# Low parts of split weights: a scaled copy on ScalarE and an accumulating transfer in place of a subtraction

## The chip, the cores and the metric

One of the eight cores of a Trainium2 chip runs the whole program. The metric is device time in microseconds (us) of one execution; the number given is the median of three runs.

## What is computed

A decoder trunk of two layers on 512 tokens of width 1024, all in float32. Layer 0 is a conformer convolution module and a gated feed-forward block with a short causal convolution; then one shared set of keys and values is projected; layer 1 is dilated windowed attention with three branches, then a second feed-forward block. Every phase ends in a norm, a residual addition and the norm of the next phase:

```python
for i in range(DEPTH):                       # DEPTH 2, N_A 1
    h = rms_norm(x, mix_pre_g[i])
    if i < N_A:
        y = conformer_conv_module(h, cm_w_in[i], ..., cm_w_out[i], cm_b_out[i])
    else:
        y = dilated_mixture_attention(h, w_q[j], w_o[j], k_sh, v_sh)
    x = x + rms_norm(y, mix_post_g[i])
    h = rms_norm(x, ffn_pre_g[i])
    y = conv_ffn(h, ffn_w_in[i], ffn_dw[i], ffn_dw_b[i], ffn_w_out[i])
    x = x + rms_norm(y, ffn_post_g[i])
    if i == N_A - 1:
        kv = (rms_norm(x, kv_norm_g) @ w_kv).reshape(b, s, 2, N_GROUPS, N_HEADS, HEAD_DIM)
```

## The kernel before

The tokens lie along the free axis (512, often in two halves of 256), the features on partitions in eight chunks of 128. The weights come as 240 units of 128 x 1024 (sixteen of them 128 x 768). TensorE multiplies in a rounded 32-bit format, `fp32r`; to keep float32's precision every operand is split into a high part, its rounded value, and a low part, the rest, and every product is three (`mm3`): high by high, high by low, low by high. In the trace `whi` and `wlo` are the parts of a unit, `hh` and `hl` (or `uh`, `ul`, `mh`, `ml`) those of the data. The products of phases are named by their output: `cia`, `cig` (conformer in), `fi`, `fo` (feed-forward in, out), `kq`, `v` (keys and queries, values), `wo` (attention out).

Who makes the parts of a unit: `loader` has SyncE fetch the unit into a buffer `raw` as soon as the buffer's last unit has its low part; there are two such buffers. `splitter` has ScalarE round `raw` into `whi` (`CAST`), and then VectorE or GpSimd subtract, `wlo` = `raw` - `whi`. GpSimd is taken when the planner's clock has it done sooner and no norm is under way (`self.chains`). There are seven places for `whi` and `wlo` (RING), and a unit is split up to six ahead of the one in use (AHEAD), but not before TensorE has done with the unit seven before it. The first two units are split in pieces by `first_units`.

The order on all five engines is written by hand-made planning while the program is built: the products of the phases are emitted in a main stream, and chains of other work (evictions, norms, splitting of weights) join it when a rough clock (`Clock`, with a cost for each instruction; `Meter` keeps it up to date) says that their operands stand and their engine is about to be free. So a different cost or a different instruction changes the order in which everything near it stands, on TensorE as well.

The norm between phases (`Junction`) runs per half of the tokens: ScalarE evicts the products as `y` and squares them (`sq`), GpSimd and VectorE add the squares up (`yacc`), TensorE sums over partitions (`st`), VectorE makes `var`, GpSimd raises it to the power -1/2 (`rst`), TensorE spreads that (`bc`), VectorE makes `t` = `y` x gain x `bc` and `x` = `x` + `t`, ScalarE makes `hh` and VectorE `hl` of the next phase. Sums of the new `x` go the same way (`xacc`, `st`, `rst`, `bc`).

Of the kernel before, what the change touches and what calls it, by code (L numbers as in the profile page):

```python
# [25 lines left out]
NEG = -1e30  # L26
RING = 7
AHEAD = 6
SEGS = [list(range(0, 6)), list(range(6, 14)), list(range(14, 22))]
# [120 lines left out]
class When:  # L150
    """The next step may go once its operands stand and the engine is about to be free."""

# [4 lines left out]
class Meter:  # L157
    """Passes calls on to an engine and keeps a rough clock of when their results stand."""

# [22 lines left out]
class Clock:  # L182
# [55 lines left out]
    def op(self, kind, name, a, k):  # L238
# [3 lines left out]
        if name == "dma_start":  # L242
# [7 lines left out]
            self.free["dma"] = s + n / 360e3  # L250
            fin = self.free["dma"] + 0.9
        else:
# [40 lines left out]
class Junction:  # L293
    """Post-norm, residual add and the operands of the next phase, one token half at a time."""

# [13 lines left out]
    def evict(self, m, p, ap, sl, mode, bias=None, sq=True, after=None, tag=0):  # L309
        """A finished chunk of y leaves PSUM; its squares are summed."""  # L310
        b, nc = self.b, self.b.nc
# [130 lines left out]
class Builder:  # L442
    def __init__(self, tc, ctx, x_d, w_d, vec_d, cvec_d, const_d, out_d):
# [47 lines left out]
        nc.sync.dma_start(self.X[0], x_d[0])  # L491
        self.raw01 = [self.wp.tile([128, 1024], F32, tag="raw", name=self.name("raw"), bufs=2) for _ in range(2)]
        for i, (o0, o1) in enumerate(PIECES):
# [6 lines left out]

    # ---- order of emission: the tensor engine's stream leads, chains of other work join when they are due
    @property
# [47 lines left out]
    def step(self, what):  # L550
        """The main stream waits: time goes on to the next chain that is due."""
        assert self.sides, what
        t = min(s.due(self.clock) for s in self.sides)
        self.now = max(self.now, t)
        assert self.now < self.t + 1000.0 and self.now < 5000.0, what
        self.advance(self.pick(max(t, self.t)))
# [6 lines left out]
    def hold_for(self, *aps):  # L563
        """Chains that are due before the operands stand go first."""
        while self.sides:
            t = self.clock.ready(*aps)
            d = min(s.due(self.clock) for s in self.sides)
            if self.t >= t or d >= t:
                break
            self.step("hold")  # L570
# [4 lines left out]
    def warm(self, out, n):  # L575
        """Products of zeros before the first real ones: the tensor engine's clock is gated down while it idles."""
        for _ in range(n):
            self.nc.tensor.matmul(out[:, :256], self.zero[:, :128], self.zero, start=True, stop=True)

    # ---- tiles  # L580
    def name(self, s):
# [36 lines left out]

    # ---- weights
    def hold(self, specs):  # L620
        """These units stay open until they are released: their products come in several passes."""
        self.held |= {self.index[s] for s in specs}
# [13 lines left out]
    def loader(self):  # L636
        nc = self.nc
        late = [(self.cst0, self.const_d[:, :160]), (self.vec, self.vec_d[:, NVA:]), (self.cst, self.const_d[:, 160:])]
        for u in range(2, len(self.order)):
            yield from self.until(("lo", u - 2))  # L640
            yield At(self.lo_done[u - 2])
            w = self.width(u)
            self.raw[u] = raw = self.wp.tile([128, 1024], F32, tag="raw", name=self.name("raw"), bufs=2)
            self.clock.hold("sp", self.lo_done[u - 2])
            nc.sync.dma_start(raw[:, :w], self.w_d[u, :, :w])
            self.mark(("raw", u))
            if u >= LATE and late:
                nc.sync.dma_start(*late.pop(0))

    def splitter(self):  # L650
        """High parts come from the Activation engine, low parts from whichever of two engines has them sooner."""
        nc, free = self.nc, self.clock.free
        for u in range(2, len(self.order)):
            while u > self.cur + AHEAD or u - RING >= self.oldest or ("raw", u) not in self.flags:
                yield 0.1
            self.next_unit = u
            raw, w = self.raw.pop(u), self.width(u)
            yield When("act", max(self.clock.ready(raw[:, :w]), self.unit_done.get(u - RING, 0.0)), SLACK)
            hi = self.wp.tile([128, 1024], F32R, tag="whi", name=self.name("whi"))
            lo = self.wp.tile([128, 1024], F32R, tag="wlo", name=self.name("wlo"))  # L660
            self.clock.hold("act", self.unit_done.get(u - RING, 0.0))
            nc.scalar.copy(hi[:, :w], raw[:, :w])
            yield self.rdy(hi[:, :w])
            at = self.clock.ready(hi[:, :w])
            if not self.chains and max(free["pool"], at) + w / 476.0 + POOL_BIAS < max(free["dve"], at) + w / 960.0:
                eng = nc.gpsimd
            else:
                eng = nc.vector
                yield self.when("dve", hi[:, :w])
            eng.tensor_tensor(lo[:, :w], raw[:, :w], hi[:, :w].bitcast(F32), op=ALU.subtract)  # L670
            self.lo_done[u] = self.clock.ready(lo[:, :w])
            self.split[self.order[u]] = (hi, lo)
            self.mark(("lo", u))
# [4 lines left out]
    def first_units(self, i):  # L678
        """One piece of the first two units, whose loads are cut so that the first products start early."""
        nc = self.nc  # L680
# [18 lines left out]

    # ---- products  # L700
    def mm3(self, out, wh, wl, xh, xl, start, stop):
# [52 lines left out]

    # ---- statistics
    def sums(self, p, o, accs, blocks):
# [5 lines left out]
    def stat(self, r, acc, blocks, rest=None):  # L762
        """r = (mean square + eps) ** -0.5 of the tokens in the blocks."""
        nc, nb = self.nc, len(blocks)
# [25 lines left out]

    # ---- conformer module
    def conv_taps(self, w_idx, Ts):
        """Banded blocks of the depthwise kernel for tokens taken four at a time."""
        nc = self.nc
# [123 lines left out]
    def stat_acc(self, CO, L):  # L918
        """Sums of the centred channels and of their squares, chunk by chunk as they come."""
        nc = self.nc  # L920
# [362 lines left out]

    # ---- feed-forward
    def ffn(self, layer, Jin, Jout):
# [95 lines left out]

    # ---- attention
    def proj_evict(self, g, p, R, t):
# [330 lines left out]
    def reload(self, src):  # L1714
        """The residual stream comes back from memory: its place was needed for other things."""
        self.X = [self.c2("x") for _ in range(KC)]
        for c in range(KC):
            self.nc.sync.dma_start(self.X[c], src[c])
# [6 lines left out]
class Chunks:  # L1725
    """Operand pairs looked up when they are needed."""

# [109 lines left out]
```

## Time and profile before

| | before |
|---|---|
| runs, us | 1523.43, 1523.62, 1525.43 (median 1523.62) |
| span of the profiled execution, us | 1520.0 |
| TensorE busy | 1484.2 us, 98% |
| VectorE busy | 941.5 us, 62% |
| ScalarE busy | 603.5 us, 40% |
| GpSimd busy | 355.7 us, 23% |
| DMA | 139.78 MB, mean 92 GB/s |
| mean granted clock of TensorE | 0.991 |

The span is what the profiler saw between the first and the last instruction, the runs are timed without it and hold a few microseconds more. Busy times of different engines overlap. A row of instructions names the line, the engine, the operation, output and inputs, the size of a tile and how often; in brackets stands how long the engine was idle before, and whose result it then had. Line 168 is a helper that records every instruction, so nearly all rows have it, and names tell the work apart.

### The profile page before, as it was taken

To read this page: it belongs to the slowest core of one execution; us is meant where nothing else is said; L and a number is where in the kernel's file an instruction comes from. 1 tells how busy PE (TensorE), PEld (TensorE's weight loads), DVE (VectorE), ACT (ScalarE), POOL (GpSimd) and SP (SyncE) were. 2 spreads that over 40 slices of the span, in tenths; PEclk is the share of its full clock that TensorE was granted. 3 is DMA by queue.
4 is the path that set the end of the run, shared out by engine and by line. 5 is a ranking of instruction groups with operands and counts; after the bars stand their busy time and mean duration, and the time that the engine had idled before them with its cause. 6 is when DMAs were issued, how large, how long until landed. Compare 5 with 4: busy or idle time off the path is not lost.

```text
span 1520.0 us, 19689 instructions
## 1 busy us (share of the span) xinstructions
PE 1484.2 (98%) x7778; PEld 1277.0 (84%) x7778; DVE 941.5 (62%) x1366; ACT 603.5 (40%) x1020; POOL 355.7 (23%) x231
## 2 busy tenths in 40 slices
PE   7999999999999998999999999999999999999997
PEld 5889998888888888889888889888898888888887
DVE  7997867846754757722655622566568746754745
ACT  5465564443432425424222323233356334422423
POOL 5885223301210216300000000000044302210213
PEclk9999999999999999999999999999999999999998
DMA  5430322233232322432222232222222332322311
GB/s 183 159 105 29 98 84 84 87 122 97 92 101 84 97 70 86 143 106 96 70 77 77 70 97 84 81 73 70 97 84 84 97 125 84 97 97 91 101 45 56
DMA packets 46892, 139.78 MB, mean 92 GB/s; under 512 B 5072, under 2 KB 10960, under 8 KB 46800
## 3 DMA queue, kind: packets, MB, share of 16 engines
q1 hardware_dynamic: 42768, 135.38, 27.4%
q10 hardware_dynamic: 4032, 3.15, 0.7%
q8 instruction: 61, 1.00, 0.3%
q14 instruction: 31, 0.25, 0.1%
HBM read 132.74 MB, written 5.77 MB: 91 GB/s over the span
## 4 chain that ended last, share of the span: by engine, by line
PE 83%; DVE 5%; ACT 1%; issue 1%; POOL 1%; DMA 0%; POOLq 0%; DVEq 0%; ACTq 0%
PE fi L168 31%; PE kq L168 17%; PE fo L168 16%; PE v L168 9%; PE wo L168 5%; PE sc L168 2%; DVE hl L168 1%; DVE mc L168 1%; DVE x L168 1%; PE pw L168 1%; PE pt L168 1%; PE pv L168 1%; DVE t L168 1%; PE cim L168 1%; PE st L168 0%
## 5 line engine op out<-in xcount | busy, mean ns | idle before, releaser
L168 ACT CAST whi<-raw 128x1024 fp32r<-128x1024 f32 (+2 forms) x242 | 248.2, 1027 | 552.8 <-PE fi L168 175.4
L168 POOL TENSOR_TENSOR wlo<-raw,whi 128x1024 fp32r<-128x1024 f32 (+1 forms) x79 | 190.8, 2416 | 985.8 <-ACT whi L168 975.6
L168 DVE TENSOR_TENSOR wlo<-raw,whi 128x1024 fp32r<-128x1024 f32 (+2 forms) x163 | 206.8, 1269 | 169.0 <-ACT whi L168 168.4
L168 PE MATMUL fi<-hl,whi 128*128 128x512 f32 (+1 forms) x768 | 289.9, 377 | 2.2 <-DVE hl L168 2.2
L168 PE MATMUL fi<-hh,whi 128*128 128x512 f32 (+1 forms) x768 | 290.8, 379 | 0.0
L168 PE MATMUL fi<-hh,wlo 128*128 128x512 f32 (+1 forms) x768 | 289.6, 377 | 0.0
L168 PEld LDWEIGHTS fi<-hl,whi 128*128 128x128 f32 x768 | 145.5, 189 | 31.4 <-DVE hl L168 2.6
L168 PEld LDWEIGHTS fi<-hh,wlo 128*128 128x128 f32 x768 | 145.5, 189 | 28.7
L168 PEld LDWEIGHTS fi<-hh,whi 128*128 128x128 f32 x768 | 145.6, 190 | 28.5
L168 PE MATMUL kq<-hh,whi 128*128 128x512 f32 (+1 forms) x416 | 164.5, 396 | 0.0
L168 PE MATMUL kq<-hh,wlo 128*128 128x512 f32 (+1 forms) x416 | 156.9, 377 | 0.0
L168 PE MATMUL kq<-hl,whi 128*128 128x512 f32 (+1 forms) x416 | 156.7, 377 | 0.0
L168 PE MATMUL fo<-uh,whi 128*128 128x512 f32 (+1 forms) x416 | 150.1, 361 | 0.0
L168 PE MATMUL fo<-uh,wlo 128*128 128x512 f32 (+1 forms) x416 | 149.7, 360 | 0.0
L168 PE MATMUL fo<-ul,whi 128*128 128x512 f32 (+1 forms) x416 | 149.7, 360 | 0.0
L168 DVE SCALAR_TENSOR_TENSOR cc<-z,vec,cc 128x511 f32<-128x511 f32 (+1 forms) x176 | 139.4, 813 | 7.0 <-ACT cc L168 4.3
L168 DVE TENSOR_TENSOR z<-fi,R 128x512 f32<-128x512 f32 x88 | 60.2, 689 | 98.3 <-PE fi L168 96.2
L168 PEld LDWEIGHTS kq<-hh,wlo 128*128 128x128 f32 x416 | 78.3, 188 | 15.5
L168 DVE TENSOR_TENSOR kq<-kq,R 128x512 f32<-128x512 f32 x48 | 46.1, 969 | 70.0 <-PE kq L168 69.3
L168 PEld LDWEIGHTS fo<-ul,whi 128*128 128x128 f32 x416 | 78.3, 188 | 13.1
L168 PEld LDWEIGHTS fo<-uh,whi 128*128 128x128 f32 x416 | 78.3, 188 | 13.0
L168 DVE TENSOR_TENSOR ul<-cc,uh 128x512 fp32r<-128x512 f32 x44 | 75.0, 1705 | 22.7 <-ACT uh L168 22.5
(212 smaller groups left out, 2631.6 us busy)
## 6 DMA issues: line engine op xcount, KB each, us to landing
raw<-in_w_dram SPq DMA_DIRECT2D x222, 512.0 KB, 3.5
raw<-in_w_dram SPq DMA_DIRECT2D x18, 384.0 KB, 3.1
x<-in_x_dram SPq DMA_DIRECT2D x16, 256.0 KB, 4.4
xs<-x SPq DMA_DIRECT2D x8, 256.0 KB, 2.7
x<-xs SPq DMA_DIRECT2D x8, 256.0 KB, 5.1
out_dram<-x SPq DMA_DIRECT2D x16, 128.0 KB, 1.8
ud<-u ACTq DMA_DIRECT2D x3, 256.0 KB, 2.0
ug<-ud ACTq DMA_DIRECT2D x3, 256.0 KB, 3.3
```

What stands on the lines that cost most here:

```text
L168: return f(*a, **k)
```

## The change

For each unit from the third on, ScalarE first writes the negative of the rounded unit into `wlo` (a copy with scale -1 into the `fp32r` buffer), then the rounded unit into `whi` as before. GpSimd then issues a DMA that adds `raw` to `wlo` in memory, so that `wlo` = `raw` - rounded `raw`. The choice between VectorE and GpSimd is gone, and with it the condition on norms under way. `raw` has four buffers in place of two, so the loader waits for the low part of the unit four before. In the planner's clock a DMA that GpSimd issues stands 2.0 us after its bytes, others 0.9 as before. Docstrings and comments that went too are left out here; they move line numbers (the helper is line 169 after).

```diff
+RAWS = 4
...
-            fin = self.free["dma"] + 0.9
+            fin = self.free["dma"] + (0.9 if kind != "pool" else 2.0)
...
-        self.raw01 = [self.wp.tile([128, 1024], F32, tag="raw", name=self.name("raw"), bufs=2) for _ in range(2)]
+        self.raw01 = [self.wp.tile([128, 1024], F32, tag="raw", name=self.name("raw"), bufs=RAWS) for _ in range(2)]
...
-            yield from self.until(("lo", u - 2))
-            yield At(self.lo_done[u - 2])
+            if u >= RAWS:
+                yield from self.until(("lo", u - RAWS))
+                yield At(self.lo_done[u - RAWS])
...
-            self.clock.hold("sp", self.lo_done[u - 2])
+            self.clock.hold("sp", self.lo_done.get(u - RAWS, 0.0))
...
             self.clock.hold("act", self.unit_done.get(u - RING, 0.0))
+            nc.scalar.activation(lo[:, :w], raw[:, :w], AF.Copy, scale=-1.0)
             nc.scalar.copy(hi[:, :w], raw[:, :w])
-            yield self.rdy(hi[:, :w])
-            at = self.clock.ready(hi[:, :w])
-            if not self.chains and max(free["pool"], at) + w / 476.0 + POOL_BIAS < max(free["dve"], at) + w / 960.0:
-                eng = nc.gpsimd
-            else:
-                eng = nc.vector
-                yield self.when("dve", hi[:, :w])
-            eng.tensor_tensor(lo[:, :w], raw[:, :w], hi[:, :w].bitcast(F32), op=ALU.subtract)
+            yield self.when("pool", lo[:, :w], slack=0.0)
+            nc.gpsimd.dma_start(lo[:, :w], raw[:, :w], accum_op=ALU.add)
```

The planner writes a new order. Three places of it follow; a row names line, operation, output and inputs with buffer numbers, and the shape.

TensorE before, in the norm between the attention's output product (`wo`) and the second feed-forward block (`fi`): the spread `bc` of the first token half stands between products of `wo`.

```order
L168 MATMUL wo_9418<-mh_8941,wlo_8969 128x256
L168 MATMUL wo_9418<-mh_8945,whi_8968 128x256
L168 MATMUL wo_9418<-ml_8946,whi_8968 128x256
L168 MATMUL wo_9418<-mh_8945,wlo_8969 128x256
L168 MATMUL bc_9424<-cst_75,rst_9385 128x128 x2
L168 MATMUL wo_9418<-mh_8949,whi_8968 128x256
L168 MATMUL wo_9418<-ml_8950,whi_8968 128x256
```

TensorE after, at the end of the same `wo`.

```order
L169 MATMUL wo_9618<-ml_9366,whi_9418 128x256
L169 MATMUL wo_9618<-mh_9365,wlo_9419 128x256
L169 MATMUL st_9691<-ones,yacc_9096 128x1 x2
L169 MATMUL st_9693<-ones,yacc_9096 128x1 x2
L169 MATMUL bc_9702<-cst_75,rst_9690 128x128 x2
L169 MATMUL bc_9707<-cst_75,rst_9692 128x128 x2
L169 MATMUL fi_9663<-hh_9721,whi_9431 128x256
L169 MATMUL fi_9663<-hl_9722,whi_9431 128x256
```

Both halves' sums and spreads have moved behind the last product of `wo`; before, the first half's `st` stood 51 products ahead of that end and the second half's 24 products behind it.

ScalarE before, at the same norm: evictions of `wo` (`y`) and squares; the last 512-wide one, `y_8914`, stands early, when the second halves of the later chunks are still to come.

```order
L168 CAST whi_9326<-raw_9263 128x1024
L168 COPY y_8914<-wo_9115 128x512
L168 COPY y_8918<-wo_9302 128x256
L168 CAST whi_9350<-raw_9287 128x1024
L168 ACTIVATE sq_9362<-y_8918 128x256
L168 ACTIVATE sq_9367<-y_8914 128x512
L168 COPY y_8915<-wo_9340 128x256
```

ScalarE after, the end of the evictions of `wo`.

```order
L169 COPY y_9094<-wo_9581 128x256
L169 ACTIVATE wlo_9630<-raw_9486 128x1024
L169 CAST whi_9629<-raw_9486 128x1024
L169 ACTIVATE sq_9667<-y_9094 128x256
L169 ACTIVATE sq_9669<-y_9088 128x512
L169 COPY y_9095<-wo_9618 128x256
L169 ACTIVATE sq_9673<-y_9089 128x512
L169 ACTIVATE sq_9676<-y_9095 128x256
L169 COPY y_9090<-wo_9240 128x512
L169 COPY y_9091<-wo_9293 128x512
L169 ACTIVATE sq_9682<-y_9090 128x512
L169 ACTIVATE sq_9684<-y_9091 128x512
```

The 512-wide evictions `y_9090` and `y_9091` and their squares have moved behind the last chunk's second half.

GpSimd before, at the norm between the conformer and the first feed-forward block.

```order
L168 TENSOR_TENSOR rst_2283<-var_2295,mhalf 128x2
L168 TENSOR_TENSOR wlo_2384<-raw_2307,whi_2383 128x1024
L168 TENSOR_TENSOR xacc_2281<-xacc_2281,sq_2397 128x256
L168 TENSOR_TENSOR xacc_2281<-xacc_2281,sq_2421 128x256
L168 TENSOR_TENSOR xacc_2281<-xacc_2281,sq_2427 128x256
```

GpSimd after, there.

```order
L169 DMA wlo_2294<-raw_1887 128x1024
L169 DMA wlo_2331<-raw_2147 128x1024
L169 TENSOR_TENSOR rst_2343<-var_2350,mhalf 128x2
L169 DMA wlo_2390<-raw_2306 128x1024
L169 TENSOR_TENSOR xacc_2341<-xacc_2341,sq_2441 128x256
L169 TENSOR_TENSOR xacc_2341<-xacc_2341,sq_2472 128x256
```

Issues of transfers now stand ahead of the first `rst` and directly behind it; four stand in a row ahead of it, two of them shown.

## Rows read from the trace of the kernel before

**Rows 1.** The page's busy times by engine, and costliest groups of instructions.

```profile
PE 1484.2 (98%) x7778; PEld 1277.0 (84%) x7778; DVE 941.5 (62%) x1366; ACT 603.5 (40%) x1020; POOL 355.7 (23%) x231
...
L168 ACT CAST whi<-raw 128x1024 fp32r<-128x1024 f32 (+2 forms) x242 | 248.2, 1027 | 552.8 <-PE fi L168 175.4
...
L168 DVE TENSOR_TENSOR wlo<-raw,whi 128x1024 fp32r<-128x1024 f32 (+2 forms) x163 | 206.8, 1269 | 169.0 <-ACT whi L168 168.4
```

**Rows 2.** Busy time by stretch: start:end, length, PE, PEld, DVE, ACT, POOL busy, PEclk, DMA share, GB/s.

```profile
210.00:250.00 40.00, 37.02 (x288) 36.61 (x287) 30.73 (x61) 19.89 (x47) 17.38 (x19) 0.91 0.21 67
250.00:580.00 330.00, 330.00 (x1449) 268.80 (x1448) 206.81 (x225) 127.42 (x164) 67.09 (x29) 1.00 0.30 96
1120.00:1160.00 40.00, 35.30 (x283) 33.79 (x281) 33.44 (x61) 20.70 (x46) 21.65 (x22) 1.00 0.23 74
```

**Rows 3.** Timeline near 16 us, VectorE and then GpSimd: start, us, engine, operation.

```profile
15.36 0.74 DVE L168 SCALAR_TENSOR_TENSOR hl<-x,vec,hh 128x512 fp32r<-128x512 f32 x1
...
16.63 2.92 DVE L168 SCALAR_TENSOR_TENSOR hl<-x,vec,hh 128x512 fp32r<-128x512 f32 x1
...
16.62 2.38 POOL L168 TENSOR_TENSOR wlo<-raw,whi 128x1024 fp32r<-128x1024 f32 x1 [2.33 <-ACT whi L168]
```

**Rows 4.** Timeline of the start: TensorE, and last ScalarE.

```profile
19.61 0.50 PE L168 MATMUL cig<-hl,whi 128*128 128x512 f32 x1 [1.65 <-DVE hl L168]
...
23.05 0.50 PE L168 MATMUL cig<-hl,whi 128*128 128x512 f32 x1 [1.79 <-DVE hl L168]
...
26.16 0.39 PE L168 MATMUL cig<-hh,wlo 128*128 128x512 f32 x1
...
15.51 1.03 ACT L168 CAST whi<-raw 128x1024 fp32r<-128x1024 f32 x1
```

**Rows 5.** Timeline of TensorE at the norm near 605 us.

```profile
603.21 0.61 PE L168 MATMUL st<-ones,yacc 128*128 128x1 f32 x4 [2.67 <-DVE yacc L168]
```

**Rows 6.** Busy time by stretch behind the norm near 230 us.

```profile
230.00:235.00 5.00, 4.25 (x21) 4.13 (x21) 2.71 (x8) 0.21 (x1) 2.10 (x4) 0.52 0.32 110
235.00:240.00 5.00, 5.00 (x36) 5.00 (x36) 4.50 (x10) 3.18 (x10) 2.29 (x3) 0.79 0.00 0
```

**Rows 7.** Timeline of ScalarE near the end of `wo`.

```profile
1107.23 1.05 ACT L168 CAST whi<-raw 128x1024 fp32r<-128x1024 f32 x1 [5.12 <-PE wo L168]
...
1112.22 0.67 ACT L168 ACTIVATE sq<-y 128x512 f32<-128x512 f32 x1
...
1115.20 0.59 ACT L168 COPY y<-wo 128x512 f32<-128x512 f32 x1
...
1118.91 0.38 ACT L168 COPY y<-wo 128x256 f32<-128x256 f32 x1 [0.72 <-PE wo L168]
...
1119.32 0.42 ACT L168 ACTIVATE sq<-y 128x256 f32<-128x256 f32 x1
...
1128.38 0.51 ACT L168 ACTIVATE hh<-x,vec 128x256 fp32r<-128x256 f32 x1
```

**Rows 8.** Timeline of GpSimd there.

```profile
1119.93 1.29 POOL L168 TENSOR_TENSOR yacc<-yacc,sq 128x512 f32<-128x512 f32 x1 [1.92 <-DVE yacc L168]
```

**Rows 9.** Timeline of VectorE there.

```profile
1123.66 0.87 DVE L168 SCALAR_TENSOR_TENSOR t<-y,vec,bc 128x256 f32<-128x256 f32 x2
...
1131.49 0.41 DVE L168 TENSOR_TENSOR x<-x,t 128x256 f32<-128x256 f32 x1
```

**Rows 10.** Timeline of TensorE there.

```profile
1113.19 0.28 PE L168 MATMUL wo<-mh,wlo 128*128 128x256 f32 x1
...
1121.28 0.27 PE L168 MATMUL st<-ones,yacc 128*128 128x1 f32 x1
...
1128.09 0.28 PE L168 MATMUL fi<-hh,whi 128*128 128x256 f32 x1
```

**Rows 11.** DMA queue and transfers, 250 to 580 us: packets, MB, share; count, KB, us to landing.

```profile
q1 hardware_dynamic: 8902, 31.39, 29.7%
...
raw<-in_w_dram SPq DMA_DIRECT2D x54, 512.0 KB, 3.5
```

More of the change, by code (lines that the diff above doesn't have):

```diff
@@ L639, in loader @@
         for u in range(2, len(self.order)):
-            yield from self.until(("lo", u - 2))
-            yield At(self.lo_done[u - 2])
+            if u >= RAWS:
+                yield from self.until(("lo", u - RAWS))
+                yield At(self.lo_done[u - RAWS])
             w = self.width(u)
-            self.raw[u] = raw = self.wp.tile([128, 1024], F32, tag="raw", name=self.name("raw"), bufs=2)
-            self.clock.hold("sp", self.lo_done[u - 2])
+            self.raw[u] = raw = self.wp.tile([128, 1024], F32, tag="raw", name=self.name("raw"), bufs=RAWS)
+            self.clock.hold("sp", self.lo_done.get(u - RAWS, 0.0))
             nc.sync.dma_start(raw[:, :w], self.w_d[u, :, :w])
```

## The prediction

> **What bounds the kernel now.** I read first the busy time by engine, then busy time by stretch, then the waits of TensorE where it is not full, then what the other engines do beside those waits. TensorE is busy 1484.2 of 1520.0 us, ScalarE 603.5, GpSimd 355.7 [rows 1]: TensorE has 35.8 us to give in all, and nothing done to another engine can gain more. By stretch [rows 2] it is full for all 330 us of the first feed-forward block's steady part, and idle at the norms between phases. I call these J1 (conformer to first FFN, near 230 us), J2 (first FFN to keys, near 605) and J3 (output projection w_o to second FFN, near 1128); the start is a fourth such place. In a full stretch the low parts are made six units ahead, and who makes them is indifferent as long as they arrive. So the change is decided at those four places, and by whether the new transfers fit in the full stretches.
>
> **What the change takes away.** The subtractions: 163 on VectorE (206.8 us) [rows 1] and the rest on GpSimd, 238 of 242 in all. In full stretches this buys nothing. At the idle places it does, because a GpSimd subtraction slows VectorE beside it: `hl` takes 0.74 us alone and 2.92 beside a GpSimd `wlo` [rows 3].
>
> Start: TensorE waits for `hl` behind that slowing twice, 1.65 + 1.79 = 3.4 us [rows 4], and both should go. What is late next is unit 2's low part, wanted at 26.16 and so at 22.7 after that gain; its negative is written where its `whi` is today, from 15.51 to 16.5 [rows 4], which leaves 6.2 us for the transfer. **Term: -3.4** (bounds -3.4, and +2 if the transfer takes 11 us).
>
> J1 and J2: TensorE is idle for 40 - 37.02 = 2.98 us at J1 [rows 2], and waits 2.67 us for one `st` at J2 [rows 5]. VectorE loses its subtractions there (1.27 us each by the mean [rows 1]), but GpSimd now issues transfers ahead of the `rst` on which each norm waits, and each transfer waits for ScalarE's negative. I count half: **-1.5 at J1, -1.3 at J2**. Bounds: at J1 the granted clock falls behind the waits, to 0.52 and 0.79 of full in ten us [rows 6], which costs 5 x 0.48 + 5 x 0.21 = 3.4 us. If the waits go, this goes too, so J1 lies between -6.4 and +2 (three `rst` late by 0.7 us each); J2 between -2.7 and +1.
>
> **What it adds on ScalarE.** 238 more passes over 128x1024. The trace has no such negation; the nearest row is the `whi` copy of that size, 1027 ns [rows 1]: about 244 us, ScalarE 604 to 848 us of 1520. In full stretches six units of lead cover it (6 x 5.3 us of TensorE's work in the FFN). At J3 nothing does, and there the order has changed too. Before, the first token half's `st` and `bc` stand between products of w_o, so that most of that half's norm is done when w_o ends; after, both halves' `st` and `bc` stand behind the last w_o product, and ScalarE has its last 512-wide evictions and squares behind three more pairs of negative and high part.
>
> **J3 worked out.** ScalarE's durations [rows 7]: a pair 2 x 1.05; `y` 0.59 (512 wide) or 0.38; `sq` 0.67 or 0.42. From the eviction that follows the end of chunk m4 (1118.91) its queue after reads: y, pair, yacc, y, pair, sq, y, pair, sq, sq (512), y, sq (512), sq, two y (512), two sq (512). The pairs cannot go earlier, since each waits for a slot that the chunk just ended frees. The sum is 3 x 2.10 + 4 x 0.38 + 4 x 0.42 + 4 x 0.67 + 2 x 0.59 = 13.4 us: 1132.3. GpSimd adds the last two squares at 1.29 us each [rows 8], the first of them from 1131.6: 1134.2. From the `st` (1121.28 [rows 10]) over `var`, `rst` and `bc` to the first `t` (1123.66 [rows 9]) took 2.4 us; then t, t, x (0.87 + 0.41 [rows 9]) and the first `hh` (0.51 [rows 7]): first `fi` product near 1138.4. It stood at 1128.09 [rows 10]: **+10.3**. Against it: the second half's `st` and `bc` no longer come later, -0.7 (0.5 for an `st` as in the step from 1121.28 to the next product, 0.2 for a `bc`, estimates). And 40 - 35.30 = 4.7 us of waits [rows 2] follow the first `fi` before; they are for the second half's norm and for `hl` beside subtractions; I take -2.7 of them. For it: TensorE is idle for some 11 us, longer than the 3 us after which it ran at about half clock at J1, so the same 3.4 us. **J3: 10.3 - 0.7 - 2.7 + 3.4 = +10.3**, bounds +4 (ScalarE meets less queueing than I count, and the clock stays) and +15 (all the waits stay as well).
>
> **What it adds on the DMA engines.** 238 accumulating transfers of 512 KB between buffers of the core, which no row shows. Price: a load of that size takes 29.7% of 330 us / 62 loads = 1.58 us of all 16 engines, and 3.5 us to landing [rows 11], so 1.9 fixed and one pass of 1.58. An accumulation reads the target too: two passes are the nearest guess (3.2 us of the engines, 5.1 to landing), one the lower bound, three the upper (4.7 and 6.7). TensorE uses 330 / 62 = 5.32 us per unit there; beside the load's 1.58, 3.74 us are free: two passes fit, three do not. I take two. Its landing shows at one place: w_o's last unit is turned from 1107.23 to 1108.28 [rows 7] and its low part wanted at 1113.19 [rows 10], 4.9 us: **+0.2** (0 to +1.8).
>
> The Trainium skill, "DMA: Bandwidth & Descriptors", section "Anatomy of one DMA — SWDGE (gpsimd) path", gives a DMA issued by GpSimd 2.0 us plus its bytes at 436 GB/s, for 512 KB an estimate of 3.2 us; by it this last term is 0 and the sum 0.2 us lower. The skill's "Collectives: The Full Stack", section "The bandwidth ceiling: the fold count and why AG ≠ RS ≠ AR", says that an adding DMA runs at about half the rate of a copy, because it reads two sources and not because adding costs time. By it two passes are right; no trace of before shows it.
>
> **Sum.** -3.4 - 1.5 - 1.3 + 10.3 + 0.2 = +4.3 us on a span of 1520.0: 1524.3. The median of the runs, 1523.62, lies 3.6 above the span, so 1527.9 us, 0.3% slower. Four raw buffers let loads run further ahead; none of the waits named here is for a load, so nothing for that.
>
> **Rivals.** 0.2% (3.05 us) is about what a measurement of this kernel cannot tell from no change: bounds 1520.6 and 1526.7.
>
> *Relief wins (not slower).* One mechanism: without GpSimd's subtractions VectorE's chain at each place runs at its undisturbed durations. Full price: start -3.4, J1 -6.4 with its clock, J2 -2.7, together -12.5. With J3 and the landing as worked out the sum is -2.0, 1521.6: same. It is faster if J3 costs half as much, +5: -7.3, 1516.3. It decides at whether ScalarE's last square at J3 ends nearer 1126 or 1132. For it: [rows 3] shows a slowing by four times. Against it: the norm's `st` has moved out of the products.
>
> *Transfers bind.* Three passes: 1.58 + 4.74 = 6.3 us per unit against 5.32, +1.0 for each unit of the FFNs, +61 in the 330-us stretch alone; two such blocks of 68 units give +136, so near 1664. It decides at 3.74 us of the engines per unit. Against it: the loads take only 0.30 of them [rows 2].
>
> *GpSimd's queue.* A transfer's issue waits for a negative that waits for TensorE's slot, and a norm's `rst` behind it waits too. If this costs six `rst` of the norms a pair and a half each, 3.1 us, that is +19 where I counted -2.8: about 1550. For it: transfers now stand between the norms' steps at J1, where only one subtraction did. Against it: most slots are free by then.
>
> **Chances and range.** Forecast (1526.7 to 1540) 0.44; GpSimd's queue 0.06; transfers bind 0.10; relief that only makes up for J3 0.20; relief that wins by more than 0.2% 0.20. Slower 0.60, same 0.20, faster 0.20. For 8 in 10 I leave out the binding transfers, the far end of the queue and the best of the relief: 1512 to 1545.
>
> **What would show it.** Right: at the start no wait for `hl` after unit 1's; at J3 one wait of 9 to 12 us at the first `st` behind w_o, with ScalarE's `sq` last, and the granted clock below full after it; full stretches still full with a DMA share of 0.6 to 0.9. Wrong: TensorE waiting for `wlo` in the FFN (transfers bind), or for `rst` with GpSimd held at an issue (queue), or a first `fi` that comes less than 5 us after w_o's end (J3 overestimated).

## The result and the profile after

The changed kernel takes 1543.86 us (median of four runs, 1540.43 to 1551.37) against 1524.53 for the kernel before beside it: a ratio of 1.0131, interval 1.0104 to 1.0159. The forecast was 1527.9 us in a range of 1512 to 1545. The sign was right, the size was a quarter of what came: +4.3 forecast, +19.3 measured. The time lies 1.1 us inside the range and 3.9 us beyond 1540, where the forecast's own stretch ended. The profile is of the fastest of the four runs.

The page of the changed kernel: busy times, the new transfers' queue, ScalarE's negatives, GpSimd's issues, and the two kinds of transfer with the time to landing. They answer to [rows 1] and [rows 11].

```profile
PE 1489.0 (97%) x7778; PEld 1280.3 (83%) x7778; DVE 656.3 (43%) x1209; ACT 819.0 (53%) x1261; POOL 354.3 (23%) x389
...
q0 software_dynamic: 34272, 122.70, 44.4%
...
L169 ACT ACTIVATE wlo<-raw 128x1024 fp32r<-128x1024 f32 (+1 forms) x238 | 248.4, 1044 | 448.0 <-PE fi L169 142.6
...
L169 POOL DMA_DIRECT2D wlo<-raw x238 | 207.2, 871 | 1070.1 <-ACT wlo L169 1031.4
...
raw<-in_w_dram SPq DMA_DIRECT2D x222, 512.0 KB, 4.7
...
wlo<-raw POOLq DMA_DIRECT2D x222, 512.0 KB, 5.9
```

VectorE fell from 941.5 to 656.3 us. ScalarE rose from 603.5 to 819.0, where the prediction had 848. The sum of the durations of its rows did rise by 244 us (657.2 to 901.2), but rows that follow one another directly overlap by some 0.1 us (the first negative ends at 16.54, the next row starts at 16.45), and busy time counts an overlap once. TensorE's busy time rose by 4.8 for the same 7778 products, at a mean granted clock of 0.982 in place of 0.991. A load of 512 KB now lands in 4.7 us in place of 3.5 (medians).

TensorE's three longest waits after: total, times, longest.

```profile
PE cv L169 <- DMA ug<-ud: 11.3, 2, 9.5
PE st L169 <- POOL yacc L169: 10.6, 1, 10.6
PE st L169 <- POOL xacc L169: 3.6, 3, 1.9
```

The wait of `st` for `yacc` is the one foretold at J3 ("one wait of 9 to 12 us at the first `st` behind w_o"). The first, of `cv` (the conformer's convolution) for `ug`, stands in no line of the prediction.

Where the time went is read off TensorE's own stream: the start of the first product of each kind, or the end of the last, in both traces. Each row's change is the difference of this and the row above it.

| TensorE reaches | before | after | difference | change in this stretch | predicted |
|---|---|---|---|---|---|
| first `cv` | 50.48 | 57.83 | +7.35 | +7.35 | -3.4 |
| last `cm` (conformer, near its end) | 169.07 | 177.87 | +8.80 | +1.45 | 0 |
| first `fo`, first block (J1 is past) | 306.01 | 310.21 | +4.20 | -4.60 | -1.5 |
| last `fo`, first block | 597.33 | 602.62 | +5.29 | +1.09 | 0 |
| first `v` (J2 is past) | 646.20 | 650.12 | +3.92 | -1.37 | -1.3 |
| last `wo` | 1128.25 | 1133.11 | +4.86 | +0.94 | +0.2 |
| first `fo`, second block (J3 is past) | 1215.30 | 1234.68 | +19.38 | +14.52 | +10.3 |
| last product | 1511.45 | 1529.73 | +18.28 | -1.10 | 0 |

So J2 came out as forecast, J1 gave three times the gain, J3 cost 4 us more, and the start cost 7.35 where 3.4 were to be won. The start's waits for `hl`, 1.65 and 1.79 us in [rows 4], are indeed gone; they were overtaken by something larger.

J1 after, in the same columns as the first row of [rows 2]:

```profile
210.00:250.00 40.00, 37.89 (x317) 37.38 (x317) 26.19 (x60) 30.31 (x60) 20.75 (x25) 1.00 0.81 194
```

TensorE is still idle there for 2.11 us (2.98 before), but the granted clock stays at 1.00.

The start after, by stretch: length, PE, PEld, DVE, ACT, POOL busy, granted clock, DMA share, GB/s.

```profile
24.00:32.00 8.00, 8.00 (x41) 6.51 (x41) 0.16 (x1) 0.00 (x0) 1.03 (x1) 1.00 1.04 245
32.00:40.00 8.00, 8.00 (x36) 6.48 (x35) 4.25 (x6) 7.64 (x9) 3.86 (x5) 1.00 0.90 254
40.00:48.00 8.00, 8.00 (x36) 6.41 (x34) 8.00 (x12) 5.51 (x8) 6.01 (x8) 1.00 0.98 234
48.00:56.00 8.00, 0.31 (x2) 0.00 (x0) 7.69 (x11) 5.23 (x7) 7.94 (x9) 0.66 1.02 242
```

And the steps behind `cv` there, TensorE's spread `bc`, ScalarE, its DMA queue (ACTq) and TensorE: start, us, engine, operation, idle before and releaser. The rows of before follow them.

```profile
26.05 0.65 PE L169 MATMUL bc<-cst,rst 128*128 128x128 f32 x4
...
32.33 1.06 ACT L169 ACTIVATE wlo<-raw 128x1024 fp32r<-128x1024 f32 x1 [9.16 <-DMA raw<-in_w_dram]
...
34.23 0.57 ACT L169 COPY R<-bc 128x512 f32<-128x512 f32 x1
...
45.06 0.35 ACTq L169 DMA_DIRECT2D ud<-u  x1
...
50.54 0.38 ACTq L169 DMA_DIRECT2D ug<-ud  x1
...
57.83 1.41 PE L169 MATMUL cv<-ug,T 128*128 128x128 f32 x5 [9.52 <-DMA ug<-ud]
```

```profile
30.46 0.59 ACT L168 COPY R<-bc 128x512 f32<-128x512 f32 x1 [6.28 <-PE bc L168]
...
32.99 1.03 ACT L168 CAST whi<-raw 128x1024 fp32r<-128x1024 f32 x1
...
41.27 0.35 ACTq L168 DMA_DIRECT2D ud<-u  x1
...
43.93 0.38 ACTq L168 DMA_DIRECT2D ug<-ud  x1
```

The DMA engines are full from 24 us on (shares 1.04, 0.90, 0.98, 1.02), although TensorE has work until 48. Unit 6's load takes 9.05 us to land (23.25 to 32.31), ScalarE stands idle for it for 9.16 us, and the copy of `R` behind that unit's pair in ScalarE's queue comes at 34.23 (30.46 before). `R` needs only `bc`, which was done at 26.7: it waits for the load because the new order puts it behind unit 6, where before it stood ahead of unit 5's high part (32.99). Through `R` go the evictions `zg` and `u`, and `u` goes out to memory and back in another arrangement (`ud`, `ug`) by two transfers in ScalarE's own queue. `ud` lands in 5.45 us in place of 2.64. `ug` was issued at 43.93 before, at 50.54 after, and lands in 7.16 us in place of 3.30. So it landed 10.5 us later (57.70, 47.23 before): 3.8 us through ScalarE's queue, 6.7 through the two transfers. Before, it had 3.2 us to spare; now `cv` waits for it for 9.52 us.

The third norm after: ScalarE, GpSimd, TensorE.

```profile
1130.90 1.06 ACT L169 ACTIVATE wlo<-raw 128x1024 fp32r<-128x1024 f32 x1 [3.08 <-DMA raw<-in_w_dram]
...
1134.96 1.06 ACT L169 ACTIVATE wlo<-raw 128x1024 fp32r<-128x1024 f32 x1 [1.49 <-DMA raw<-in_w_dram]
...
1139.72 1.16 ACT L169 ACTIVATE sq<-y 128x512 f32<-128x512 f32 x2
...
1141.08 2.60 POOL L169 TENSOR_TENSOR yacc<-yacc,sq 128x512 f32<-128x512 f32 x2 [0.60 <-DVE yacc L169]
...
1143.73 1.87 PE L169 MATMUL st<-ones,yacc 128*128 128x1 f32 x8 [10.62 <-POOL yacc L169]
...
1148.31 0.58 PE L169 MATMUL fi<-hh,whi 128*128 128x256 f32 x1 [1.00 <-ACT hh L169]
```

This is the chain that the prediction worked out, ScalarE's last squares, GpSimd's last sums, `st`. But ScalarE waits twice for a load, 3.08 and 1.49 us, which no row of before had at this place. By stretch, the same columns as above:

```profile
1130.00:1135.00 5.00, 3.11 (x27) 2.90 (x25) 0.42 (x1) 2.61 (x5) 0.86 (x1) 1.00 1.05 305
1135.00:1140.00 5.00, 0.00 (x0) 0.00 (x0) 0.42 (x1) 5.00 (x10) 2.91 (x3) 0.60 1.06 264
1140.00:1145.00 5.00, 1.27 (x6) 1.27 (x7) 0.58 (x2) 0.89 (x2) 3.00 (x3) 0.50 0.75 227
1145.00:1150.00 5.00, 3.27 (x11) 2.09 (x12) 3.65 (x11) 2.25 (x5) 2.04 (x3) 0.50 0.04 16
1150.00:1155.00 5.00, 5.00 (x33) 5.00 (x32) 4.80 (x11) 4.01 (x10) 4.42 (x6) 0.70 0.55 105
```

The DMA engines are full here too (1.05, 1.06; the two loads took 8.88 and 8.05 us to land), and the granted clock goes to 0.50, the lower of the two levels (1.2 of 2.4 GHz), for as long as TensorE has little to do, and some us beyond. That fall was foretold at 3.4 us.

In the steady part of the first block TensorE remains full, with the new queue's share of the 16 engines first and the stretch behind it:

```profile
q0 software_dynamic: 8889, 31.30, 54.3%
```

```profile
260.00:590.00 330.00, 330.00 (x1461) 267.56 (x1461) 129.75 (x193) 180.84 (x228) 53.29 (x62) 1.00 0.83 189
```

54.3% of 330 us for the 61 transfers of the stretch (eight of them three quarters long, so 59 whole ones) is 3.04 us of the engines each. The forecast took 3.2 from "two passes" of a load's 1.58. That 1.58 counts eight short loads as whole; by 60 whole ones in [rows 11] a load is 1.63. The Trainium skill's "Collectives: The Full Stack", section "The bandwidth ceiling: the fold count and why AG ≠ RS ≠ AR", says of rings between cores that the reducing step runs at about half the rate of the copying one, because its add needs two source reads; the trace agrees for this transfer within one core, 3.04 us against 1.63 for a load.

### The profile page after: what moved, and what is told of

It is laid out like the page before. It is cut to its first block, busy times and chain, and to the rows that moved or that the text cites. A ratio compares the mean times of both kernels' runs of the same rounds, so it can differ in the third digit from the quotient of the medians.

```text
span 1538.7 us, 20030 instructions
## 1 busy us (share of the span) xinstructions
PE 1489.0 (97%) x7778; PEld 1280.3 (83%) x7778; DVE 656.3 (43%) x1209; ACT 819.0 (53%) x1261; POOL 354.3 (23%) x389
## 3 DMA queue, kind: packets, MB, share of 16 engines
q0 software_dynamic: 34272, 122.70, 44.4%
## 4 chain that ended last, share of the span: by engine, by line
PE 73%; issue 11%; DVE 6%; DMA 4%; ACT 3%; POOL 2%; SPq 0%; POOLq 0%; ACTq 0%; DVEq 0%
PE fi L169 31%; PE fo L169 16%; PE kq L169 10%; PE v L169 9%; PE wo L169 3%; DMA raw<-in_w_dram 2%; DMA wlo<-raw 1%; POOL wlo L169 1%; DVE u L169 1%; DVE x L169 1%; DVE hl L169 1%; PE sc L169 1%; PE cm L169 1%; PE cim L169 1%; DVE t L169 1%
## 5 line engine op out<-in xcount | busy, mean ns | idle before, releaser
L169 ACT ACTIVATE wlo<-raw 128x1024 fp32r<-128x1024 f32 (+1 forms) x238 | 248.4, 1044 | 448.0 <-PE fi L169 142.6
L169 POOL DMA_DIRECT2D wlo<-raw x238 | 207.2, 871 | 1070.1 <-ACT wlo L169 1031.4
L169 ACT CAST whi<-raw 128x1024 fp32r<-128x1024 f32 (+2 forms) x242 | 244.7, 1011 | 1.7 <-DMA raw<-in_w_dram 1.7
L169 PEld LDWEIGHTS fi<-hh,whi 128*128 128x128 f32 x768 | 146.1, 190 | 29.9 <-ACT hh L169 1.4
L169 DVE SCALAR_TENSOR_TENSOR cc<-z,vec,cc 128x511 f32<-128x511 f32 (+1 forms) x176 | 128.2, 749 | 91.2 <-ACT cc L169 88.4
L169 PEld LDWEIGHTS kq<-hl,whi 128*128 128x128 f32 x416 | 79.4, 191 | 11.8
```

The source lines that it names most:

```text
L169: return f(*a, **k)
```

## The experiments

Two theories for the two large losses. **D**: the adding transfers fill the DMA engines where units are turned faster than in the feed-forward blocks, so loads and gathers come late. **S**: ScalarE's longer queue, and the order that the planner made of it, holds up what TensorE waits for.

**A plain transfer in place of the adding one.** The order of the work remains as it is.

```diff
-            nc.gpsimd.dma_start(lo[:, :w], raw[:, :w], accum_op=ALU.add)
+            nc.gpsimd.dma_start(lo[:, :w], raw[:, :w])
```

> The changed kernel with the adding transfer made a plain transfer of the same bytes; every instruction stands in the same order. It leaves out the subtraction: the low part is then a copy of the raw weight. Theory D (the losses at the start and at the third norm come from DMA engines that are full, share 1.0): the transfer's price falls from 2.9 to about 1.6 us of the 16 engines, the wait of cv for ug shrinks from 9.5 us to under 3, the wait of st for yacc behind w_o from 10.6 to 5 to 7, and the time to 1524 to 1530 us. Theory S (they come from ScalarE's longer queue and the order of the work): both waits stay within 1.5 us of what they were, 1538 to 1545 us.

1518.99 us, ratio 0.9967 (0.9954 to 0.9979): faster than the kernel before. TensorE's longest wait, the stretch of the late load and the one in which `cv` begins, and the queue's share of the whole span (44.4% with the add):

```profile
PE st L169 <- POOL yacc L169: 6.2, 1, 6.2
```

```profile
24.00:32.00 8.00, 8.00 (x42) 6.54 (x41) 1.81 (x4) 4.88 (x6) 2.65 (x3) 1.00 0.98 334
...
48.00:56.00 8.00, 8.00 (x53) 7.16 (x52) 7.26 (x11) 5.05 (x8) 7.62 (x8) 1.00 0.79 248
```

```profile
q0 software_dynamic: 34272, 122.70, 22.8%
```

The wait for `ug` is gone and `cv` starts at 48.85, 1.6 us ahead of the kernel before. At the first `fi` this kernel is 8.18 us ahead, where the changed kernel is 7.47 behind: in the conformer the add in place of a plain transfer costs 15.7 us. The share of the DMA engines does not tell the two apart from 24 to 32 us (0.98 here, 1.04 with the add); what they moved does, 334 GB/s against 245. Unit 6's load lands at 27.07 here, `ud` and `ug` in 2.92 and 4.83 us. So D holds there. S alone costs nothing at this place, since ScalarE's queue is the same in both; but with a late load that queue is the way by which the delay reaches `R`, and the adding transfers with `R` ahead of unit 6 were not run. The edit has a second effect, GpSimd's time at each issue, 0.54 us in place of 0.87; but near the start GpSimd waits for ScalarE's negative before nearly every issue in both kernels. At J3 the wait falls from 10.62 to 6.20 us, and ScalarE no longer waits for a load there. From the last `wo` to the first `fi` passed 15.20 us in the changed kernel, 10.78 here and nothing before (-0.16). So 4.4 us of J3 are D, about the two waits for loads (4.57), and some 10.9 are S: the size that the prediction had worked out for it. The expected time of theory D was 1524 to 1530; that it is lower still shows how large the relief in the conformer would be if the transfers cost nothing more than a copy.

**The negative on VectorE.** ScalarE does what it did before; the DMA engines carry the same bytes.

```diff
-            nc.scalar.activation(lo[:, :w], raw[:, :w], AF.Copy, scale=-1.0)
             nc.scalar.copy(hi[:, :w], raw[:, :w])
+            yield self.when("dve", raw[:, :w])
+            nc.vector.tensor_scalar(lo[:, :w], raw[:, :w], -1.0, None, op0=ALU.mult)
```

> The changed kernel with the negative written by VectorE (a multiplication by -1, behind whi) in place of ScalarE; the planner then again puts the first half's st and bc between products of w_o. Theory S: the third norm costs no more than before (first fi within 2 us of w_o's end) and the gather at the start waits under 3 us: 1522 to 1528 us. Theory D: the DMA engines carry the same bytes, so cv still waits 7 us or more for ug and the third norm still has a loss of 4 us or more: 1532 to 1540 us.

1553.32 us, ratio 1.0187 (1.0162 to 1.0213), slower than either theory said. TensorE's longest waits:

```profile
PE cv L169 <- DMA ug<-ud: 19.6, 2, 11.4
...
PE bc L169 <- POOL rst L169: 5.3, 4, 3.2
```

The wait of `st` behind w_o is no longer there: the first `fi` follows the last `wo` at once (-0.16 us, as before the change). So S holds at J3: with ScalarE's load taken back the planner puts the norm among the products again. But theory D's loss of 4 us or more is there as well, ahead of that end: w_o's products run some 28.3 us behind the kernel before and end 33.1 behind. In between `bc`, among the products again, waits 3.17 us for `rst`; its `var` stands in VectorE's queue behind a negative whose load took 8.46 us to land, and `rst` in GpSimd's behind the issue of a transfer.

```profile
1153.04 0.69 DVE L169 TENSOR_SCALAR wlo<-raw 128x1024 fp32r<-128x1024 f32 x1 [0.38 <-DMA raw<-in_w_dram]
...
1155.68 0.69 PE L169 MATMUL bc<-cst,rst 128*128 128x128 f32 x2 [3.17 <-POOL rst L169]
```

At the start `cv` waits for the gather for longer, 11.36 and 8.21 us, and the loss at the end of the conformer is 29.9 us. But the first gather lands quickly here, `ud` in 2.72 us and `ug` in 3.79. Late is its issue, 56.29 for `ud` (41.27 before):

```profile
38.74 1.05 ACT L169 CAST whi<-raw 128x1024 fp32r<-128x1024 f32 x1 [6.87 <-DMA raw<-in_w_dram]
...
38.74 0.69 DVE L169 TENSOR_SCALAR wlo<-raw 128x1024 fp32r<-128x1024 f32 x1 [6.09 <-DMA raw<-in_w_dram]
```

A load that took 11.06 us to land holds ScalarE and VectorE at once, with the convolution's operands behind it in both queues. So D holds for the load, and the new place of the negatives carries it further. The miss in size has a part that I leave open: the order at the start moved too, as TensorE's wait of 4.1 us for unit 2's low part shows.

**Two raw buffers in place of four.**

```diff
-RAWS = 4
+RAWS = 2
```

> The changed kernel with two raw buffers in place of four. If the buffers set the pace: a buffer is taken for a load (4.7 us), the two passes of ScalarE (2), the issue (0.9) and the adding transfer (5.9), 13.5 us for two units or 6.7 us a unit, against the 5.3 us in which TensorE uses a unit of the feed-forward blocks: about +1.4 us on each of 136 units, near 1730 us, with TensorE waiting for wlo. If transfers of different units overlap enough that only the engines' share counts (4.45 us a unit), the feed-forward blocks stay full and the time is 1535 to 1550 us.

1610.61 us, ratio 1.0571 (1.0555 to 1.0587), between the two expectations. TensorE's longest wait, and rows of ScalarE and TensorE in the first block:

```profile
PE fo L169 <- ACT uh L169: 25.0, 4, 8.0
```

```profile
324.30 0.84 ACT L169 ACTIVATE wlo<-raw 128x768 fp32r<-128x768 f32 x1 [2.08 <-DMA raw<-in_w_dram]
...
326.44 0.80 PE L169 MATMUL fo<-uh,whi 128*128 128x512 f32 x1 [6.19 <-ACT uh L169]
```

The first block takes 27 us more than in the changed kernel (first `fo` to last `fo`, some 54 units), 0.5 us per unit, not 1.4: the two chains overlap more than I counted. But the price is paid by ScalarE, which waits for a load with other work behind it in its queue. TensorE waits for the data's own high part (`uh`), 25.0 us over the two blocks, and for `wlo` only once, 3.4 us. The rest of the loss is spread over the attention, the second block and J3 (`st` waits 21.2 us).

**The kernel before with four raw buffers.**

```diff
+RAWS = 4
...
-            yield from self.until(("lo", u - 2))
-            yield At(self.lo_done[u - 2])
+            if u >= RAWS:
+                yield from self.until(("lo", u - RAWS))
+                yield At(self.lo_done[u - RAWS])
```

> The kernel before with four raw buffers in place of two, and nothing else. If buffers matter by themselves (loads that run further ahead collide with the gather at the start, or feed the splitting sooner), the first cv or the conformer's end moves by over 2 us; my view is that no wait of before is for a load, so within 1.5 us of before, 1522 to 1526 us.

1530.21 us, ratio 1.0034 (1.0014 to 1.0053). A miss, if a small one: buffers alone cost 5.1 us by the medians. The ten runs spread from 1524.48 to 1536.29, and the profile is of one of the fastest (1524.81), so the trace shows 2.8 of it. The first `cv` moves by 1.0; the last `cm` comes 4.15 us earlier, which J1 gives back with 1.1 more (`st` waits there 4.62 us for `yacc`); and 2.1 are lost in the norm at J3, where the order has changed.

**Subtraction again for the conformer, w_o and eight units at J3.** 200 units keep the adding transfer.

```diff
+    def by_dma(self, u):
+        return self.order[u][0] not in ('cin', 'cout', 'o') and not 0 <= u - self.index[('fi', 1, NF)] < 8
...
+            if self.by_dma(u):
                 nc.scalar.activation(lo[:, :w], raw[:, :w], AF.Copy, scale=-1.0)
                 nc.scalar.copy(hi[:, :w], raw[:, :w])
                 yield self.when("pool", lo[:, :w], slack=0.0)
                 nc.gpsimd.dma_start(lo[:, :w], raw[:, :w], accum_op=ALU.add)
+            else:
...
```

> The changed kernel, but the conformer's units, those of w_o and the first eight of the second feed-forward block get their low parts by subtraction on VectorE or GpSimd as before (200 units keep the adding transfer). Both theories: the losses at the start (+8.8 us) and at the third norm (+14.5) go, the gains at the first norm (-4 to -5 us) and the second (-1.4) stay: 1515 to 1522 us, a little faster than before. If the gain at the first norm came from the conformer's own units, it is gone too and the time is 1522 to 1526 us.

1524.65 us, ratio 0.9996 (0.9983 to 1.001): both losses are gone and nothing is won. Between the first `fi` and the first `fo` 3.9 us are still gained (+2.67, then -1.24 against before), but the conformer ends 2.7 us late, and J3's second half loses 2.1 us, as with four buffers alone.

**All units but the first ten of the conformer, w_o and eight at J3.**

```diff
-        return self.order[u][0] not in ('cin', 'cout', 'o') and not 0 <= u - self.index[('fi', 1, NF)] < 8
+        return u >= 10 and self.order[u][0] != 'o' and not 0 <= u - self.index[('fi', 1, NF)] < 8
```

> Adding transfers for all units but the first ten, those of w_o and the first eight of the second feed-forward block (214 units). Theory D (only the filling of the ring at the start, where loads, gathers and adding transfers meet, is too much for the DMA engines): the conformer's steady part gains what the plain transfers showed, its end lies 3 us or more ahead of the kernel before, and the time is 1514 to 1520 us. Rival: in the whole conformer the transfers delay the gathers (ud, ug), and the first feed-forward block begins no sooner than before: 1521 to 1528 us.

1533.41 us, ratio 1.0054 (1.0035 to 1.0074). It is the rival: six more units of the conformer by adding transfer, and TensorE waits for the gather again, with 10.4 us lost at the first `fi`.

```profile
57.30 0.98 PE L169 MATMUL cv<-ug,T 128*128 128x128 f32 x3 [4.02 <-DMA ug<-ud]
...
92.45 0.93 PE L169 MATMUL cv<-ug,T 128*128 128x128 f32 x5 [3.71 <-DMA ug<-ud]
```

The filling of the ring is thus not the only place; where the gathers run, a few adding transfers beside them are enough.

**All but the conformer's first product, w_o and eight at J3.**

```diff
-        return self.order[u][0] not in ('cin', 'cout', 'o') and not 0 <= u - self.index[('fi', 1, NF)] < 8
+        return self.order[u][0] not in ('cin', 'o') and not 0 <= u - self.index[('fi', 1, NF)] < 8
```

> Adding transfers for all units but the conformer's sixteen of the first product, those of w_o and the first eight of the second feed-forward block (208 units): against the hybrid with 200 it gives the eight units of the conformer's second product back to the transfers. If the gain at the first norm comes from these and the following units, the first fi stands 1 to 4 us ahead of the kernel before and the time is 1517 to 1522 us; if not, as that hybrid, 1523 to 1526 us.

1520.09 us, ratio 0.997 (0.9958 to 0.9983). Eight units of the conformer's second product (208 units now) are worth 5 us at the first `fi`, which stands 2.37 us ahead of before where the variant with 200 units was 2.67 behind.

**Adding transfers for 39 units.** 31 of them are split around the first two norms. The condition on `fo` names no block, so the last eight `fo` units of the second block are among the 39 too (issued from 1423.5 to 1477.2 us).

```diff
-        return self.order[u][0] not in ('cin', 'cout', 'o') and not 0 <= u - self.index[('fi', 1, NF)] < 8
+        return 16 <= u < 32 or self.order[u][0] == 'fo' and self.order[u][2] == 2 or self.order[u][0] in ('k', 'q') and u < 110
```

> Adding transfers for 39 units alone: those split around the first norm (conformer's second product, first eight of the first feed-forward block) and the second (last eight of that block, first of the keys). If the full stretches are indifferent to who makes the low parts, it keeps the gains at both norms like the variant with 208 and the time lies within 2 us of that; if the transfers also help or hurt within the full stretches, the two differ by more.

1516.22 us, ratio 0.9939 (0.9919 to 0.996): **0.6% ahead of the kernel before**, and ahead of the changed one. It is 3.9 us ahead of the 208 units, which is outside the 2 us of the expectation. But TensorE's stream agrees with theirs within about 1 us at every landmark, and its last product ends at the same time (1504.81 and 1504.73). So the full stretches are indifferent to about 1 us, as the prediction said. The span is 2.9 us shorter behind that last product, and there GpSimd's longest `DRAIN`, which the program's end waits for, takes 4.14 us in place of 7.12 (the longest of three durations, in ns; 208 units first, then 39):

```profile
L1838 POOLq DRAIN x3: 34/93/7125, 1509.4 to 1517.0; - x3
```

```profile
L1838 POOLq DRAIN x3: 34/102/4144, 1509.5 to 1514.1; - x3
```

It takes 0.94 us before, 3.08 in the changed kernel and 6.47 with 200 units. What sets it is open. J1 in this kernel, to be held against the first row of [rows 2]:

```profile
210.00:250.00 40.00, 38.60 (x297) 36.87 (x296) 30.52 (x63) 28.53 (x56) 19.96 (x24) 1.00 0.71 171
```

38.60 of 40 us busy, and the granted clock stays at 1.00 where it fell to 0.91 before.

**The same with two, and with three raw buffers.**

```diff
-RAWS = 4
+RAWS = 2
```

> The 39-unit variant with two raw buffers, as the kernel before has. The order at the third norm is then that of the kernel before. If the four buffers cost the second half of that norm the 3 us that the kernel before with four buffers lost there, and the 39 units do not need them, 1512 to 1516 us; if the adding transfers at the first two norms are then late (a buffer is held 13.5 us for two units, as with two buffers throughout), the gain at the first norm shrinks by 2 us or more and the time is 1517 to 1522 us.

1538.91 us, ratio 1.0086 (1.0066 to 1.0105). The same stretch, then ScalarE's and TensorE's rows in it:

```profile
210.00:250.00 40.00, 35.27 (x263) 34.86 (x262) 26.88 (x59) 28.59 (x59) 19.95 (x24) 0.87 0.74 171
```

```profile
219.06 1.06 ACT L169 ACTIVATE wlo<-raw 128x1024 fp32r<-128x1024 f32 x1 [1.90 <-DMA raw<-in_w_dram]
```

```profile
231.70 0.58 PE L169 MATMUL fi<-hh,wlo 128*128 128x256 f32 x1 [3.60 <-DMA wlo<-raw]
```

ScalarE waits for a load whose buffer an adding transfer still held (it landed at 214.28, the load was issued at 214.35), and TensorE for the low part. The first norm loses, 9.0 us by the first `fo`, and the second loses as much again (`st` waits 6.3 us, first `v` +18.2). J3 is in order, with nothing lost there against before. The second expectation, but with a price far beyond it.

```diff
-RAWS = 4
+RAWS = 3
```

> The 39-unit variant with three raw buffers: between the variants with two and with four. If both effects of the buffers are real (order at the third norm, late transfers at the first), within 3 us of the better of the two: 1513 to 1518 us.

1541.55 us, ratio 1.0101 (1.0079 to 1.0124). A miss: not between the two but beside the worse. Its losses lie elsewhere in the conformer (`lst` waits 7.5 us for GpSimd) and at J2 (`st` waits 7.7 us), with an order of its own. Ahead of J2 ScalarE waits 8.75 us for a load (7.37 with two buffers) that was issued when an adding transfer let go of its buffer and took 8.17 us to land beside two more. What part of the rest is the buffers' and what the order's is open.

## Why the prediction was right and where it failed

**In the range, and partly by luck.** The errors of the terms partly cancel: the start came out 10.8 us above its term and J3 4.2, J1 3.1 below, and 3.3 us were lost in stretches that the prediction put at nothing or nearly so, with a gain of 1.1 at the end. The time stands 1.1 us from the end of the range, nearer to the 1550 of the queue rival than to the forecast, though the traces do not show that rival at work in this kernel.

**Right.** That the full stretches are indifferent, to about 1 us each; that the two waits for `hl` at the start go; J2 (-1.4 for -1.3); the price of a transfer in the engines (3.04 for 3.2); w_o's last unit, for which nobody waited; and above all the way of J3: the norm out of the products, ScalarE's last square late, one wait of 10.62 us, and the lower clock behind it. The plain transfer shows 10.9 us of that place without any wait for a load, where the step "J3 worked out" had +10.3 for the first `fi`. The waits after the first `fi` shrank as assumed: what follows to the first `fo` came out 0.8 us shorter, where -0.7 - 2.7 + 3.4 gives 0.

**The step that failed** is "What it adds on the DMA engines". The price was right, the test was made in one place only: "two passes fit" in 5.32 us per unit of the feed-forward block. At the start and at w_o the units are turned at the pace of ScalarE and of the buffers, about one in 2 us at the start (15.50, 17.39, 19.28, 21.18 for the first four negatives) and in 2.8 at w_o (1117.18 and 1119.95), and there 1.63 + 3.04 us per unit do not fit. The DMA share of before from 8 to 16 us, when the first loads run, is 0.99; I had looked at the share of the 330-us stretch, 0.30.

```profile
8.00:16.00 8.00, 4.97 (x18) 3.21 (x19) 7.58 (x7) 7.61 (x13) 4.73 (x4) 1.00 0.99 374
```

And I asked of the start's other transfers nothing: `ud` and `ug` are in no step, though TensorE's convolution depends on them. Nor did I ask what stands behind a load in the queue of the engine that waits for it ("none of the waits named here is for a load"): `R` at the start, the squares at J3. The start's term was 10.8 us off (+7.35 for -3.4), the largest error.

**J3's bound.** The same cause: two waits for loads, 4.6 us in ScalarE's chain. The plain transfer gives 4.4 of the 15.2 us between `wo` and `fi` to the add.

**J1, -4.6 for -1.5.** I counted half of the waits and let the fall of the clock stand. The waits shrank by 0.9 us only (2.98 to 2.11 of 40 us); what went is the fall of the clock, 3.4 us in the prediction's bounds (the granted clock stays at 1.00). So the term that was mis-sized is the clock's. GpSimd's queue, the rival with `rst` behind a transfer, cost little: TensorE waited 2.2 us in all for `rst`, 5.2 before.

**The buffers.** "So nothing for that" was wrong twice: alone they cost 0.3% (2.1 us of it at J3, where the 39 units lose 2.9), and with adding transfers they are needed, since a buffer is held until the transfer has landed.

## What to carry to other kernels

Price a transfer against the DMA engines in the stretch where its units come fastest, not where they come steadily, and list every other transfer in that stretch whose result somebody awaits. An engine that waits for a late load holds up everything behind it in its queue, so look there for work that another engine awaits. Where a full engine hides who does a job, move the job only at the places where it is not full: 39 units of 238 gave all of the gain at the first two norms, and lost 2.9 us at the third, where four buffers alone lose 2.1. A kernel whose order is planned from costs reacts to a new cost by a new order, so read first which waits of the old order had other work beside them.

## What the runs showed of the hardware

Over the whole span the adding transfers (238, or 234 whole ones) take 44.4% of 1538.7 us, 2.92 us of the 16 engines per 512 KB, and plain ones of the same bytes 22.8% of 1517.4 us, 1.48 us: the add costs about twice a copy. From issue to landing it takes 5.9 us (median) against 3.3 for the plain one. GpSimd is taken for 0.87 us at each adding issue and 0.54 at each plain one; the 207.2 us of the adding ones are about as much as the subtractions that it was spared (190.8).

Where the DMA engines were full, loads of 512 KB took 8 to 11 us to land (9.05 at the start, 8.88 and 8.05 at J3, 11.06 with VectorE's negative), against 3.5 in the kernel before. A share near 1.0 does not say how much is moved: 334 GB/s with plain transfers, 245 with adding ones, in the same 8 us of the start.
